# SSD scan: the decay matrix and x as rounded halves, and the state product in the state bank

## The chip, the cores and the metric

The kernel runs on one core of a Trainium2 chip. The metric is the device time of one execution in microseconds (us); lower is better. The chip's engines appear under these names: TensorE (PE; its weight loads are listed apart as PEld), VectorE (DVE), ScalarE (ACT), GpSimd (POOL) and SyncE (SP), whose queue issues most DMAs.

## What is computed

The reference is one inference step of two layers, a Mamba-2 SSD layer and a latent attention (MLA) layer, for a prompt of 1024 tokens and 8 samples of 8 tokens. The change is in the SSD scan of the prompt. For each of 8 groups (4 heads of width 64 and a shared state width of 128) it goes over 8 chunks of 128 tokens. Cut to what matters:

```python
seg = a_cs[..., :, None] - a_cs[..., None, :]
decay = jnp.where(causal, jnp.exp(jnp.where(causal, seg, 0.0)), 0.0)
cb = jnp.einsum('bclgn,bcsgn->bgcls', cc, bc)
y_diag = jnp.einsum('bgrcls,bcsgrp->bclgrp', cb[:, :, None] * decay, xdt)     # inside a chunk
states = jnp.einsum('bcsgn,bcsgrp->bcgrpn', bc, xdt * decay_end[..., None])   # what a chunk adds
# over the chunks:  state -> chunk_decay * state + states[chunk], from prev = the state before it
y_off = jnp.einsum('bclgn,bcgrpn->bclgrp', cc, prev) * decay_in[..., None]    # from earlier chunks
y = y_diag + y_off
```

After it come `y + D * x`, the gate `silu(z)`, a grouped norm and the output projection.

## The kernel before

The SSD layer projects the normalised input to z, x, B, C and dt, convolves x, B and C over time, runs the scan, and multiplies by the output weights. Matrix products that must be as exact as f32 are made of two rounded halves: `split` (L125) copies a tile to fp32r with ScalarE (L127, the high half) and subtracts that from the tile with VectorE or GpSimd (L133, the low half); `mm3` (L83) then adds three matmuls, high by high, high by low and low by high. Some products are left as plain f32 matmuls.

The groups are a pipeline: while the scan of group g runs, the projections and convolution of group g + 1 (`Group.steps`, matmuls `pj` at L86 and `pz` at L98) are issued in between. `layer_ssd` (L926 to L938) asks for the steps in proportion to the scan's progress; `ssd_scan` (L733) mixes chunks and the samples' state updates in the order `SCAN`. In the last group the first half of the output projection (`poa`) takes the place of the next group's projections. In this layer no order is written by hand: the code gives instructions in program order, and a scheduler puts them on the queues of the engines by its own estimate of time. On a queue, an instruction that waits holds up those behind it.

A chunk of `ssd_chunks` (L580) does this:

- transposes x (two blocks) and B into the bank `trp` (L594 to L597); copies x to `xsT` (L599); splits B into `Bh`, `Bl` (L602).
- makes `xdd` = x times decay to the chunk's end on GpSimd (L613) and splits it into `dh`, `dl`; splits C into `Ch`, `Cl` and the state S into `Sh`, `Sl` (L618, L620), with GpSimd for the low halves; makes `xD` = D * x (L622).
- makes the product C·B in the bank `cb` (L624).
- loads the cumulated decay into M by DMA (L626), adds the causal mask on VectorE (L627), takes the exponential for each of 4 heads on ScalarE (L630), and multiplies by C·B on VectorE (L631). M is 128 x 4 x 128.
- multiplies M of each head with 64 columns of x in plain f32 into columns 0 to 255 of the bank `py` (L635).
- adds what the chunk brings to the state in the bank `ps` (L639, columns 0 to 255), and from the second chunk on makes the product of C with the state in columns 256 to 511 of `py` (L644).
- the new state S2 is the decayed S (GpSimd, L645) plus `ps` (VectorE, L647).
- y: the state product times decay (L651), plus the first product (L652), plus `xD` (GpSimd, L653), times z (L656); in the first chunk there is no state product (L655). Then the squares are summed (L657) and y is written out (L658).

The ninth chunk of a group holds the samples (64 tokens, `smp`) and takes its state product from `ssd_states` (L669), which also uses the tags of `M` (tile xr, L685), `fo` (tile xf, L690) and the bank of `ps` (L725). Accumulator banks: `tr` 2, `pj` 2, `cb` 1, `y` 2 (tile py), `st` 1 (tile ps).

Of the kernel before, what the change touches and what calls it, by code (L numbers as in the profile page):

```python
# [8 lines left out]
F32 = mybir.dt.float32  # L9
F32R = mybir.dt.float32r  # L10
AF = mybir.ActivationFunctionType
ALU = mybir.AluOpType
# [70 lines left out]
def mm3(nc, out, pairs):  # L83
    n = len(pairs)
    for i, (a, b) in enumerate(pairs):
        nc.tensor.matmul(out, a, b, start=(i == 0), stop=(i == n - 1))  # L86
# [26 lines left out]
def open_pool(tc, name, bufs=1, space=None, **kw):  # L113
    if space is None:
        return tc.tile_pool(name=name, bufs=bufs, reuse_waits="tile", **kw)
    if space == PS:
        return tc.tile_pool(name=name, bufs=bufs, space=space, reuse_waits="tile", **kw)
    return tc.tile_pool(name=name, bufs=bufs, space=space, **kw)
# [6 lines left out]
def split(k, hi, lo, src, eng=None, parts=0):  # L125
    nc = k.nc
    nc.scalar.copy(hi, src)  # L127
    n = parts and hi.shape[1] // parts
    for a in range(parts):
        s = slice(a * n, a * n + n)  # L130
        (eng or nc.vector).tensor_tensor(lo[:, s], src[:, s], hi[:, s].bitcast(F32), op=ALU.subtract)
    if not parts:
        return (eng or nc.vector).tensor_tensor(lo, src, hi.bitcast(F32), op=ALU.subtract)  # L133
# [446 lines left out]
def ssd_chunks(k, gr, pools):  # L580
    nc, I = k.nc, k.I
    sp, psum = pools
    g = gr.g
    S = None
    hs = slice(4 * g, 4 * g + 4)
    for i in range(9):
        t0, m = TILES[i]
        sl = slice(t0, t0 + m)
        smp = i == 8
        B, C, X0, X1 = (gr.xc[q][1][:, j] if smp else gr.xc[q][0][:, j, sl] for q in range(2) for j in range(2))  # L590
        z = gr.z[i // 5][:m, i % 5]
        tag = f"{g}_{i}"
        p = psum.tile([128, 512], F32, tag="tr", name="trp" + tag, bufs=PB["tr"])
        nc.tensor.transpose(p[:m, 0:128], X0, k.ident)  # L594
        nc.tensor.transpose(p[:m, 128:256], X1, k.ident)
        if not smp:
            nc.tensor.transpose(p[:m, 256:384], B, k.ident)  # L597
        xsT = sp.tile([128, 256], F32, tag="xsT", name="xsT" + tag, bufs=2)
        nc.scalar.copy(xsT[:m], p[:m, 0:256])  # L599
        if not smp:  # L600
            Bh, Bl = (sp.tile([128, 128], F32R, tag="BT" + x, name="BT" + x + tag, bufs=2) for x in "hl")
            split(k, Bh, Bl, p[:, 256:384])  # L602
        tk = k.tok[:m, i]

        def hb(j):
            return tk[:, j, hs].unsqueeze(2).to_broadcast([m, 4, 64])

        def v3(t):
            return t[:m].rearrange("p (h q) -> p h q", q=64)

        if not smp:
            xdd = sp.tile([128, 256], F32, tag="xdd", name="xdd" + tag, bufs=1)
            nc.gpsimd.tensor_tensor(v3(xdd), v3(xsT), hb(2), op=ALU.mult)  # L613
            dh, dl = (sp.tile([128, 256], F32R, tag="xdd" + x, name="xdd" + x + tag, bufs=1) for x in "hl")
            split(k, dh, dl, xdd, nc.gpsimd)
            if S is not None:
                Ch, Cl = (sp.tile([128, 128], F32R, tag="C" + x, name="C" + x + tag, bufs=1) for x in "hl")
                split(k, Ch, Cl, C, nc.gpsimd)  # L618
                Sh, Sl = (sp.tile([128, 256], F32R, tag="S" + x, name="S" + x + tag, bufs=1) for x in "hl")
                split(k, Sh, Sl, S, nc.gpsimd)  # L620
        xD = sp.tile([128, 256], F32, tag="xD", name="xD" + tag, bufs=XDB)
        nc.gpsimd.tensor_tensor(v3(xD), v3(xsT), k.dsk[:m, hs].unsqueeze(2).to_broadcast([m, 4, 64]), op=ALU.mult)  # L622
        pc = psum.tile([128, 512], F32, tag="cb", name="cb" + tag, bufs=PB["cb"])
        nc.tensor.matmul(pc[:m, :m], B, C, start=True, stop=True)  # L624
        M = sp.tile([128, 4, 128], F32, tag="M", name="M" + tag, bufs=2)
        nc.sync.dma_start(M[:m, :, :m], (k.acss_d[hs] if smp else k.acs_d[i, hs]).partition_broadcast(m))  # L626
        nc.vector.tensor_tensor(M[:m, :, :m], M[:m, :, :m],  # L627
                                (k.negs if smp else k.negu)[:m, :m].unsqueeze(1).to_broadcast([m, 4, m]), op=ALU.add)
        for h in range(4):
            nc.scalar.activation(M[:m, h, :m], M[:m, h, :m], AF.Exp, bias=tk[:, 0, 4 * g + h : 4 * g + h + 1])  # L630
        nc.vector.tensor_tensor(M[:m, :, :m], M[:m, :, :m],  # L631
                                pc[:m, :m].unsqueeze(1).to_broadcast([m, 4, m]), op=ALU.mult)
        py = psum.tile([128, 512], F32, tag="y", name="py" + tag, bufs=PB["y"])
        for h in range(4):
            nc.tensor.matmul(py[:m, h * 64 : h * 64 + 64], M[:m, h, :m], xsT[:m, h * 64 : h * 64 + 64],  # L635
                             start=True, stop=True)
        if not smp:
            ps = psum.tile([128, 512], F32, tag="st", name="st" + tag, bufs=PB["st"])
            mm3(nc, ps[:, :256], [(Bh, dh), (Bh, dl), (Bl, dh)])  # L639
            S2 = sp.tile([128, 256], F32, tag="S", name=f"S{g}_{i + 1}", bufs=2)  # L640
            if S is None:
                nc.vector.tensor_copy(S2, ps[:, :256])
            else:
                mm3(nc, py[:m, 256:], [(Ch, Sh), (Ch, Sl), (Cl, Sh)])  # L644
                nc.gpsimd.tensor_tensor(S2.rearrange("p (h q) -> p h q", q=64), S.rearrange("p (h q) -> p h q", q=64),  # L645
                                        k.decp[:, hs, i : i + 1].to_broadcast([128, 4, 64]), op=ALU.mult)
                nc.vector.tensor_tensor(S2, S2, ps[:, :256], op=ALU.add)  # L647
            S = S2
        y = sp.tile([128, 256], F32, tag="y", name="y" + tag, bufs=YB)
        if i:  # L650
            nc.vector.tensor_tensor(v3(y), v3(gr.yo if smp else py[:, 256:]), hb(3), op=ALU.mult)  # L651
            nc.vector.tensor_tensor(y[:m], y[:m], py[:m, :256], op=ALU.add)  # L652
            nc.gpsimd.tensor_tensor(y[:m], y[:m], xD[:m], op=ALU.add)  # L653
        else:
            nc.vector.tensor_tensor(y, py[:, :256], xD, op=ALU.add)  # L655
        nc.vector.tensor_tensor(y[:m], y[:m], z, op=ALU.mult)  # L656
        nc.scalar.activation(xD[:m], y[:m], AF.Square, accum_out=k.yssq[:m, i, g : g + 1])  # L657
        nc.sync.dma_start(k.y_d[sl, 256 * g : 256 * g + 256], y[:m])  # L658
        if i == 7:
            pf = psum.tile([128, 512], F32, tag="tr", name="pf" + tag, bufs=PB["tr"])  # L660
            for pr in range(2):
                nc.tensor.transpose(pf[:, pr * 128 : pr * 128 + 128], S[:, pr * 128 : pr * 128 + 128], k.ident)
            fo = sp.tile([128, 256], F32, tag="fo", name="fo" + tag, bufs=1).rearrange("p (a n) -> p a n", a=2)
            nc.scalar.copy(fo, pf[:, :256].rearrange("p (a n) -> p a n", a=2))
            nc.sync.dma_start(k.O["p_ssm"][0, 0, 4 * g : 4 * g + 4].rearrange("(a h) p n -> (h p) a n", h=2), fo)
        yield
# [66 lines left out]
def ssd_scan(k, gr, pools):  # L733
    chunks, states = ssd_chunks(k, gr, pools), ssd_states(k, gr, pools)
    for c in SCAN:
        next(chunks if c == "c" else states)
        yield 21 / len(SCAN)
    drain(chunks)
    drain(states)
# [125 lines left out]
def layer_ssd(k):  # L865
    tc, nc = k.tc, k.nc
# [7 lines left out]
    with ExitStack() as st:  # L874
# [39 lines left out]
                pass  # L914
            ssd_dt(k, p0, psum)
        sp = right.enter_context(open_pool(tc, name="sp", bufs=2, side="right"))
        k.cblk = [sp.tile([128, 4, 64], F32R, name=f"cblk{q}") for q in range(2)]
        for t in k.cblk:
            nc.gpsimd.memset(t.bitcast(F32), 0.0)
        gr = g0  # L920
# [5 lines left out]
        for g in range(G - 1):  # L926
# [11 lines left out]
            gr = nx  # L938
# [1091 lines left out]
def hybrid_kernel(tc, ins, outs):  # L2030
    k = Ctx()
    k.tc, k.nc, k.I, k.O, k.ng = tc, tc.nc, ins, outs, G
    with ExitStack() as st:
        setup(k, st)
        layer_ssd(k)
        layer_mla(k)
# [19 lines left out]
```

## Time and profile before

| | before |
|---|---|
| median of 3 runs | 1953.28 us (1952.03 to 1955.74) |
| the profiled execution | 1949.75 us |
| span of its instructions | 1948.0 us |
| busy TensorE / VectorE / ScalarE / GpSimd | 97% / 61% / 57% / 43% of the span |
| matmul instructions | 12023 |
| bytes moved by DMA | 202.01 MB, 104 GB/s on average |

The profile is of one execution: its span is the time from the first instruction to the last, and the execution's own time lies 1.75 us above it. Times of rows are microseconds from the span's start, and durations of one instruction stand in ns where they are means of a group. A matmul's recorded duration holds its passage through the array, which overlaps with the next matmul's; what a matmul costs in a row of them is the distance from its start to the next one's. A plain f32 matmul stands as two rows. In a row of grouped instructions, the part behind the bar has the busy time, the mean duration, and the time for which the engine sat idle before them, with what ended it.

### The profile page before, as it was taken

The page shows a single profiled execution, that of the slowest core. Times are in us where ns is not written, and L with a number is a line of the kernel's source. Part 1 is how long each engine was busy: PE and PEld are TensorE (multiplying, and loading weights), DVE is VectorE, ACT ScalarE, POOL GpSimd, SP SyncE. Part 2 cuts the span into 40 slices and gives each one's busy share as a digit, 9 for nine tenths or more (in the row PEclk, how much of TensorE's full clock was granted, in tenths as well). Part 3 has the DMA queues.
Part 4 walks back from the last instruction along what each step waited for, and adds up shares of the span by engine and source line. Part 5 has one row for each costly group of instructions (what it writes and reads, how often), then busy time and mean ns, then how long its engine had stood idle before and what let it go on. Part 6 is the DMA issues. An engine that isn't in the chain of part 4 may idle for free.

```text
span 1948.0 us, 33561 instructions
## 1 busy us (share of the span) xinstructions
PE 1898.6 (97%) x12023; PEld 1732.3 (89%) x12023; DVE 1189.8 (61%) x2423; ACT 1108.4 (57%) x2535; POOL 841.3 (43%) x1122
## 2 busy tenths in 40 slices
PE   9999999999999999899999999999999999899998
PEld 7999999999999999788788998898888888778887
DVE  5566565657666656755533104476787778666564
ACT  6466666667666666732214314336777777855552
POOL 2447455555655555443003212104443434865551
PEclk9999999999999999999999999999999999999999
DMA  5123223332323332544533333133111112654431
GB/s 167 48 72 93 86 85 97 84 108 84 96 81 96 86 95 82 190 161 156 181 114 117 123 150 94 56 109 94 48 49 41 51 40 59 215 181 149 144 128 38
DMA packets 181086, 202.01 MB, mean 104 GB/s; under 512 B 18828, under 2 KB 147608, under 8 KB 180536
## 3 DMA queue, kind: packets, MB, share of 16 engines
q1 hardware_dynamic: 175864, 180.08, 30.1%
q0 software_dynamic: 4976, 19.66, 2.9%
q8 instruction: 95, 1.56, 0.3%
q14 instruction: 71, 0.58, 0.1%
q10 hardware_dynamic: 80, 0.13, 0.0%
HBM read 146.52 MB, written 53.28 MB: 103 GB/s over the span
## 4 chain that ended last, share of the span: by engine, by line
PE 82%; ACT 5%; DMA 4%; DVE 4%; POOL 3%; issue 2%; SPq 0%; POOLq 0%; DVEq 0%; ACTq 0%
PE pj L86 19%; PE pz L98 8%; PE pq L98 6%; PE pob L98 5%; PE p L98 5%; PE poa L98 5%; PE sc L86 2%; PE py L635 2%; PE o L86 2%; DMA M<-acs_d 2%; PE o L1426 2%; PE sc L1363 2%; PE o L1428 2%; PE st L1395 2%; PE st L1397 2%
## 5 line engine op out<-in xcount | busy, mean ns | idle before, releaser
L86 PE MATMUL pj<-xh,wih 128*128 128x384 f32 (+1 forms) x768 | 254.2, 335 | 0.5 <-ACT raw L512 0.3
L86 PE MATMUL pj<-xl,wih 128*128 128x384 f32 (+1 forms) x768 | 253.7, 330 | 0.0
L86 PE MATMUL pj<-xh,wil 128*128 128x384 f32 (+1 forms) x768 | 253.2, 330 | 0.0
L1409 POOL TENSOR_TENSOR tl<-P,th 128x384 fp32r<-128x384 f32 (+1 forms) x96 | 91.3, 951 | 235.1 <-ACT P L1407 188.9
L526 DVE SCALAR_TENSOR_TENSOR acc<-raw,vec,acc 128x1112 f32<-128x1112 f32 x96 | 142.2, 1482 | 26.4 <-ACT acc L522 25.4
L86 PEld LDWEIGHTS pj<-xh,wih 128*128 128x128 f32 x768 | 143.9, 188 | 2.3 <-ACT xh L273 0.8
L86 PEld LDWEIGHTS pj<-xl,wih 128*128 128x128 f32 x768 | 144.5, 188 | 1.0
L86 PEld LDWEIGHTS pj<-xh,wil 128*128 128x128 f32 x768 | 144.4, 188 | 0.4
L98 PE MATMUL pz<-wih,xh 128*128 128x256 f32 x504 | 142.8, 287 | 0.6 <-ACT z L567 0.6
L98 PE MATMUL pz<-wil,xh 128*128 128x256 f32 (+1 forms) x504 | 140.2, 284 | 0.0
L1406 ACT ACTIVATE th<-st 128x512 fp32r<-128x512 f32 x192 | 94.5, 492 | 65.5 <-PE st L1402 50.5
L630 ACT ACTIVATE M<-M,tok 128x128 f32<-128x128 f32 (+1 forms) x288 | 90.9, 386 | 66.7 <-DVE M L627 66.3
L98 PE MATMUL pz<-wih,xl 128*128 128x256 f32 x448 | 128.3, 286 | 0.0
L1699 POOL TENSOR_TENSOR kvl<-pgr,kvh 128x256 fp32r<-128x256 f32 x128 | 96.3, 779 | 66.3 <-ACT kvh L1697 65.6
L98 PEld LDWEIGHTS pz<-wih,xh 128*128 128x128 f32 x504 | 95.9, 190 | 1.3 <-ACT z L567 1.0
L627 DVE TENSOR_TENSOR M<-M,negu 128x512 f32<-128x512 f32 x64 | 52.6, 822 | 68.3 <-DMA M<-acs_d 67.9
L1407 ACT ACTIVATE P<-st 128x512 f32<-128x512 f32 x192 | 93.7, 488 | 0.0
L98 PEld LDWEIGHTS pz<-wil,xh 128*128 128x128 f32 (+1 forms) x504 | 92.7, 184 | 0.7
L133 DVE TENSOR_TENSOR wil<-wraw,wih 128x512 fp32r<-128x512 f32 x88 | 71.3, 817 | 27.6 <-ACT wih L127 24.4
L613 POOL TENSOR_TENSOR xdd<-xsT,tok 128x256 f32<-128x256 f32 x64 | 50.8, 794 | 80.5 <-ACT xsT L599 80.1
L98 PEld LDWEIGHTS pz<-wih,xl 128*128 128x128 f32 x448 | 85.2, 190 | 0.1
L1409 DVE TENSOR_TENSOR tl<-P,th 128x512 fp32r<-128x512 f32 x96 | 70.9, 739 | 18.5 <-ACT P L1407 17.6
(832 smaller groups left out, 6302.7 us busy)
## 6 DMA issues: line engine op xcount, KB each, us to landing
wraw<-in_ssd_w_in SPq DMA_DIRECT2D x92, 256.0 KB
M<-acs_d SPq DMA_DIRECT2D x64, 256.0 KB
s<-in_state_ssm SPq DMA_DIRECT2D x32, 256.0 KB
y_d<-y SPq DMA_DIRECT2D x64, 128.0 KB
out_s_ssm<-s SPq DMA_DIRECT2D x32, 256.0 KB
wraw<-in_ssd_w_out SPq DMA_DIRECT2D x12, 512.0 KB
q_d<-qt SPq DMA_DIRECT2D x32, 192.0 KB
qp<-q_d SPq DMA_DIRECT2D x8, 768.0 KB
```

The costliest lines, as they stand in the source:

```text
L86: nc.tensor.matmul(out, a, b, start=(i == 0), stop=(i == n - 1))
L98: nc.tensor.matmul(o, a, b, start=(j == 0), stop=(j == len(ops) - 1))
L133: return (eng or nc.vector).tensor_tensor(lo, src, hi.bitcast(F32), op=ALU.subtract)
L526: last = nc.vector.scalar_tensor_tensor(acc, raw[:, j : j + n], k.convw[j][:, blk : blk + 1], acc, op0=ALU.mult, op1=ALU.add)
L613: nc.gpsimd.tensor_tensor(v3(xdd), v3(xsT), hb(2), op=ALU.mult)
L627: nc.vector.tensor_tensor(M[:m, :, :m], M[:m, :, :m], (k.negs if smp else k.negu)[:m, :m].unsqueeze(1).to_broadcast([m, 4, m]), op=ALU.add)
L630: nc.scalar.activation(M[:m, h, :m], M[:m, h, :m], AF.Exp, bias=tk[:, 0, 4 * g + h : 4 * g + h + 1])
L635: nc.tensor.matmul(py[:m, h * 64 : h * 64 + 64], M[:m, h, :m], xsT[:m, h * 64 : h * 64 + 64], start=True, stop=True)
L1406: nc.scalar.activation(th[:, :n], ps[:, :n], AF.Exp, scale=SCALE)
L1407: nc.scalar.activation(P[:, :n], ps[:, :n], AF.Exp, scale=SCALE)
L1409: eng.tensor_tensor(tl[:, :n], P[:, :n], th[:, :n].bitcast(F32), op=ALU.subtract)
L1699: nc.gpsimd.tensor_tensor(rl[:, j], raw[:, j], rh[:, j].bitcast(F32), op=ALU.subtract)
```

## The change

For the 64 prompt chunks, M and x are split into rounded halves. The halves of x lie side by side for each head, so that one matmul with 128 moving columns gives M's half times both halves of x; two such matmuls (Mh, Ml) are added up in 128 columns of `py`, which is filled by the four heads. The two column blocks of each head are added when y is made. The product of C with the state goes to the free columns of `ps`, ahead of the chunk's own contribution. `xdd` shares its buffer with `xf` and `fo`, and the two tiles `cblk` get one buffer each instead of two. The samples' chunk is left as it was.

```diff
+            xhl = sp.tile([128, 4, 2, 64], F32R, tag="xhl", name="xhl" + tag, bufs=1)
+            split(k, xhl[:, :, 0], xhl[:, :, 1], p[:, 0:256].rearrange("p (h q) -> p h q", q=64))
...
-            xdd = sp.tile([128, 256], F32, tag="xdd", name="xdd" + tag, bufs=1)
+            xdd = sp.tile([128, 256], F32, tag="fo", name="xdd" + tag, bufs=1)
...
-        for h in range(4):
-            nc.tensor.matmul(py[:m, h * 64 : h * 64 + 64], M[:m, h, :m], xsT[:m, h * 64 : h * 64 + 64],
-                             start=True, stop=True)
+        pv = py.rearrange("p (h a q) -> p h a q", h=4, a=2)
+        if smp:
+            for h in range(4):
+                nc.tensor.matmul(py[:m, h * 64 : h * 64 + 64], M[:m, h, :m], xsT[:m, h * 64 : h * 64 + 64],
+                                 start=True, stop=True)
+        else:
+            Mh, Ml = (sp.tile([128, 4, 128], F32R, tag="M" + x, name="M" + x + tag, bufs=1) for x in "hl")
+            split(k, Mh, Ml, M)
+            for h in range(4):
+                nc.tensor.matmul(py[:, h * 128 : h * 128 + 128], Mh[:, h], xhl[:, h].rearrange("p a q -> p (a q)"),
+                                 start=True, stop=False)
+                nc.tensor.matmul(py[:, h * 128 : h * 128 + 128], Ml[:, h], xhl[:, h].rearrange("p a q -> p (a q)"),
+                                 start=False, stop=True)
...
             ps = psum.tile([128, 512], F32, tag="st", name="st" + tag, bufs=PB["st"])
+            if S is not None:
+                mm3(nc, ps[:, 256:], [(Ch, Sh), (Ch, Sl), (Cl, Sh)])
             mm3(nc, ps[:, :256], [(Bh, dh), (Bh, dl), (Bl, dh)])
...
-                mm3(nc, py[:m, 256:], [(Ch, Sh), (Ch, Sl), (Cl, Sh)])
...
-            nc.vector.tensor_tensor(v3(y), v3(gr.yo if smp else py[:, 256:]), hb(3), op=ALU.mult)
-            nc.vector.tensor_tensor(y[:m], y[:m], py[:m, :256], op=ALU.add)
+            nc.vector.tensor_tensor(v3(y), v3(gr.yo if smp else ps[:, 256:]), hb(3), op=ALU.mult)
+            if smp:
+                nc.vector.tensor_tensor(y[:m], y[:m], py[:m, :256], op=ALU.add)
+            else:
+                nc.vector.tensor_tensor(v3(y), v3(y), pv[:, :, 0], op=ALU.add)
+                nc.vector.tensor_tensor(v3(y), v3(y), pv[:, :, 1], op=ALU.add)
...
-            nc.vector.tensor_tensor(y, py[:, :256], xD, op=ALU.add)
+            nc.vector.tensor_tensor(v3(y), pv[:, :, 0], v3(xD), op=ALU.add)
+            nc.vector.tensor_tensor(v3(y), v3(y), pv[:, :, 1], op=ALU.add)
...
-        k.cblk = [sp.tile([128, 4, 64], F32R, name=f"cblk{q}") for q in range(2)]
+        k.cblk = [sp.tile([128, 4, 64], F32R, name=f"cblk{q}", bufs=1) for q in range(2)]
```

More of the change, by code (lines that the diff above doesn't have):

```diff
@@ L600, in ssd_chunks @@
         if not smp:
+            xhl = sp.tile([128, 4, 2, 64], F32R, tag="xhl", name="xhl" + tag, bufs=1)
+            split(k, xhl[:, :, 0], xhl[:, :, 1], p[:, 0:256].rearrange("p (h q) -> p h q", q=64))
+        if not smp:
             Bh, Bl = (sp.tile([128, 128], F32R, tag="BT" + x, name="BT" + x + tag, bufs=2) for x in "hl")
```

## The prediction

> **What bounds the kernel now.** I read the page first, then busy time by stage, then what TensorE waited for, then its instructions one by one.
>
> ```profile
> PE 1898.6 (97%) x12023; PEld 1732.3 (89%) x12023; DVE 1189.8 (61%) x2423; ACT 1108.4 (57%) x2535; POOL 841.3 (43%) x1122
> ...
> PE 82%; ACT 5%; DMA 4%; DVE 4%; POOL 3%; issue 2%; SPq 0%; POOLq 0%; DVEq 0%; ACTq 0%
> ```
>
> TensorE is busy for 97% of the span and carries 82% of the chain that ended last. A busy TensorE need not be at its peak, so the stage has to be looked at. The changed lines run in the scan, from 117 to 916 us, in three stretches:
>
> ```profile
> core 0 of [0], span 1948.0 us
> core 0: us, PE busy (x) PEld busy (x) DVE busy (x) ACT busy (x) POOL busy (x), PEclk, DMA share, GB/s
> 117.00:220.00 103.00, 97.07 (x723) 94.44 (x721) 70.77 (x118) 69.27 (x175) 66.72 (x93) 1.00 0.35 100
> 220.00:800.00 580.00, 574.49 (x4223) 562.14 (x4221) 374.75 (x621) 391.79 (x959) 324.58 (x478) 1.00 0.31 91
> 800.00:916.00 116.00, 109.99 (x625) 92.38 (x624) 72.13 (x124) 48.59 (x132) 49.00 (x69) 0.99 0.50 171
> ```
>
> TensorE idles 5.9 + 5.5 + 6.0 = 17.4 us in these 799 us; in the middle stretch it is 99% busy, at the full granted clock. VectorE has 65% there, ScalarE 68%, GpSimd 56%. What TensorE waits for between 117 and 916 us, the largest first:
>
> ```profile
> PE st L86 <- POOL xddl L133: 3.6, 2, 2.5
> PE cb L624 <- DVE yo L722: 2.0, 2, 1.0
> PE pv L719 <- DVE sl L133: 2.0, 1, 2.0
> PE sn L726 <- POOL bb L701: 1.9, 5, 0.4
> PE st L86 <- ACT xddh L127: 1.7, 2, 1.4
> ```
>
> No engine holds it back regularly. So a microsecond saved on TensorE in the scan is a microsecond of the whole, one saved elsewhere is nothing, and one added elsewhere is free as long as TensorE has other matmuls in front.
>
> **The change part by part.** First the product with the decay matrix (L635), in 64 full chunks (the 8 sample chunks keep their code). One chunk of before:
>
> ```profile
> 327.98 0.34 PE L86 MATMUL pj<-xh,wil 128*128 128x384 f32 x1
> 328.16 1.00 PE L635 MATMUL py<-xsT,M 128*128 128x64 f32 x8
> 328.96 0.36 PE L86 MATMUL st<-xddh,BTh 128*128 128x256 f32 x1
> 329.17 0.28 PE L86 MATMUL st<-xddl,BTh 128*128 128x256 f32 x1
> 329.28 0.28 PE L86 MATMUL st<-xddh,BTl 128*128 128x256 f32 x1
> ```
>
> Four f32 matmuls stand as 8 passes, each with a weight load of 128 columns. They take 0.80 us from start to start, and the matmul behind them takes 0.21 us where the next one takes 0.11, so 0.10 us more belongs to them: 0.90 us a chunk, 0.11 us a pass. The new code has eight rounded (fp32r) matmuls, Mh and Ml for four heads, also with 128 weight columns each, and 128 moving columns. The trace has such matmuls in the attention:
>
> ```profile
> 1335.72 0.27 PE L1396 MATMUL st<-qTl,kTh 98*128 98x128 f32 x1
> 1335.83 0.27 PE L1397 MATMUL st<-qTh,kTl 98*128 98x128 f32 x1
> 1335.94 0.28 PE L1402 MATMUL st<-mr 128*128 128x128 f32 x1
> 1336.06 0.44 PE L86 MATMUL kp<-kvh,w 128*128 128x512 f32 x1
> ```
>
> They start 0.11, 0.11 and 0.12 us apart, 0.113 on average, no less than the 256 columns wide ones above. Streaming doesn't explain that; the weight load does, because the same width behind narrower weights (32 and 64 columns) goes twice as fast:
>
> ```profile
> 345.87 0.22 PE L719 MATMUL pv<-sl,cblk 128*32 128x128 f32 x1
> 345.93 0.22 PE L719 MATMUL pv<-sh,cblk 128*64 128x128 f32 x1
> ```
>
> Both forms are thus bound by loads, and both have eight: 8 x 0.113 = 0.91 us after, 0.90 before. **This term is 0**; the last digits make it at most 0.02 us a chunk either way, 1.3 us in all. The matmuls of the state products keep number and shape; where they write (state bank, not y bank) costs TensorE nothing.
>
> The Trainium skill's "TensorE: Matmul & The Clock Gate", section Back-to-back issue gap, gives about 81 ns for a sustained pair of a weight load and a 128-column matmul. By it the eight would take 0.65 us, and the sum would be 64 x 0.25 = 16 us lower (estimate). The rows above, at 110 ns, disagree with it for this data type, and I go by them.
>
> Next, what the other engines get, per full chunk. The nearest rows, between 117 and 916 us:
>
> ```profile
> L599 ACT COPY xsT<-trp 128x256 f32<-128x256 f32 x64 | 24.0, 375 | 12.1 <-PE trp L597 11.7
> ...
> L652 DVE TENSOR_TENSOR y<-y,py 128x256 f32<-128x256 f32 x56 | 23.1, 413 | 0.7
> ...
> L133 DVE TENSOR_TENSOR sl<-s0p,sh 128x512 fp32r<-128x512 f32 x32 | 21.9, 685 | 7.0 <-ACT sh L127 6.9
> ...
> L127 ACT CAST sh<-s0p 128x512 fp32r<-128x512 f32 x32 | 18.5, 578 | 0.8 <-PE s0p L710 0.8
> ```
>
> ScalarE: Mh (128x512) 0.58, the high half of x (128x256) 0.38, together 0.96 us. VectorE: Ml 0.68, the low half of x 0.41, one more addition to y 0.41, together 1.50 us. Over 64 chunks: 61 us of ScalarE and 96 us of VectorE. Spread over 799 us, ScalarE goes from 510 to 571 us (71%) and VectorE from 518 to 614 us (77%). Neither becomes the bound on average; the cover is the projection matmuls of the next group, which TensorE runs meanwhile. If that cover were gone, the price would be the latency, below.
>
> The chain to the product grows: L631 (the multiplication with C·B), then Mh, then Ml, then the matmuls, two hops of 0.58 + 0.68 = 1.26 us. How early is M ready now? VectorE's rows, then TensorE's, for a common chunk and for the one with the shortest lead:
>
> ```profile
> 331.44 0.67 DVE L631 TENSOR_TENSOR M<-M,cb 128x512 f32<-128x512 f32 x1
> ...
> 549.56 0.68 DVE L631 TENSOR_TENSOR M<-M,cb 128x512 f32<-128x512 f32 x1
> ```
>
> ```profile
> 334.60 1.00 PE L635 MATMUL py<-xsT,M 128*128 128x64 f32 x8
> ...
> 551.15 1.00 PE L635 MATMUL py<-xsT,M 128*128 128x64 f32 x8
> ```
>
> The leads are 334.60 - 332.11 = 2.49 us and 551.15 - 550.24 = 0.91 us. Of the 64 leads, 7 are under 1.3 us (1.9 us short in all) and 16 under 2.0 us (9.6 us short in all, if 0.7 us of queueing is added to the two hops). The code lets the order of each engine be written anew by the scheduler, and one that knows the longer chain puts the product later, at no cost. So this term lies between 0 and 9.6 us, and I take **5 us**, the middle: rows on both sides are equally near.
>
> The state. Now ps is held through both products and the reading of both halves, in the only buffer of its tag, and B's product stands behind C's, so S_(i+1) waits for Sh and Sl of S_i, which it didn't:
>
> ```profile
> L133 POOL TENSOR_TENSOR Sl<-S,Sh 128x256 fp32r<-128x256 f32 x56 | 51.6, 922 | 4.0 <-ACT Sh L127 4.0
> ...
> L127 ACT CAST Sh<-S 128x256 fp32r<-128x256 f32 x56 | 22.4, 401 | 9.5 <-DVE S L647 9.4
> ```
>
> The loop is 0.40 + 0.92 + two products of 0.33 (three steps of 0.11) + 0.41 for the addition: 2.4 us, against 799 / 64 = 12.5 us a chunk on average and 6 to 7 us where two follow each other (328.16 and 334.60). Hidden; so is the next user of that buffer, L726's matmul, by the projections. In return the first y product no longer stands behind M's matmuls, which helps VectorE, not TensorE. The x halves (one buffer) wait for the previous product and keep the transposes' bank that much longer; ScalarE, where those copies queue, also empties the projections' banks behind them. That, and GpSimd slowed by 64 more two-operand subtractions on VectorE, no row prices; between 0 and the 5.5 us that the middle stretch idles now, I take **1 us**, near the lower end, since the middle stretch shows almost no such wait. The shared tag of xdd, the single buffer of cblk: 0. No DMA is added, and the load of the next M waits for Ml instead of the matmuls behind it, so SP's queue is not later.
>
> Sum: 0 + 5 + 1 = 6 us. The profiled execution took 1949.75 us, so 1955.8; the median of the three runs is 1953.28, so **1959 us**, +0.3%. A measurement of this kernel tells 0.2%, 3.9 us, from no change.
>
> **Rivals.**
> *All of it is covered* (same): the order is rewritten and TensorE's queue stays as full as the 99% now. Then 1953, give or take 3.9. For it: equal loads on TensorE, and a typical lead of 2.5 us. Against it: leads near 1 us.
> *The waits go away* (faster): C's product leaves M's shadow, and the waits for xdd and S, up to 3.6 + 1.7 us, vanish in the new order: 1948. The ceiling is the whole idle time of the scan, 17.4 us: 1936. Against it: nothing is taken from GpSimd, which those waits name.
> *Rounded weights load faster* (faster): at the 0.06 us of the last two TensorE rows the eight would take 0.48 us, 64 x 0.42 = 27 us off, 1926. The attention rows speak against it. By the Trainium skill's figure above it would be 1937.
> *In-order queues block* (slower): at 77% and 71% a copy of Mh that waits for VectorE stands in front of ScalarE's emptying of projection banks. It decides once TensorE is held up at every chunk: one Ml (0.68 us) a chunk is 64 x 0.68 = 44 us, 1997; half the chunks, 1975.
> *The change does nothing for TensorE* isn't a rival but the forecast's own basis.
>
> **How the numbers follow.** Forecast (slower by 4 to 12 us) 0.37, queues block 0.14, all covered 0.31, waits go away 0.14, faster loads 0.04. Slower 0.51, same 0.31, faster 0.18. The range from 1947 to 1983 leaves out the faster loads, the upper part of the vanished waits, and the blocked queues above some two thirds of the chunks, about 0.15; the likeliest case alone is 1957 to 1965.
>
> **What would show it.** Right: L635's successors at eight passes 0.11 us apart; TensorE's busy time in the scan within 1 us of before; waits of the y product for Ml (VectorE) as the new name among TensorE's waits, some 5 us; VectorE near 614 us in the scan. Wrong: starts closer than 0.1 us; waits of pj or pz for ScalarE of over 10 us (queues block); a scan shorter than 799 us with no waits for Ml.

## The result and the profile after

| | before | after |
|---|---|---|
| median of 4 runs each, in turn on one chip | 1952.65 us (1951.14 to 1955.74) | 2005.09 us (1997.36 to 2009.82) |
| ratio to before, 95% interval | | 1.0267 [1.0245, 1.029] |
| the profiled execution | 1949.75 us | 2003.53 us |
| mean granted TensorE clock | 0.996 | 0.986 |

The change makes the kernel 52 us slower; the forecast was 1959 and its range ended at 1983. From the page of the kernel after, the busy times and the chain that ended last:

```profile
PE 1921.4 (96%) x12023; PEld 1748.3 (87%) x12023; DVE 1294.3 (65%) x2615; ACT 1164.8 (58%) x2667; POOL 857.8 (43%) x1122
...
PE 65%; DVE 12%; ACT 11%; DMA 7%; issue 4%; POOL 2%; SPq 0%; DVEq 0%; ACTq 0%; POOLq 0%
```

The number of matmuls is the same, and TensorE still looks 96% busy. But its share of the chain falls from 82% to 65%; VectorE, ScalarE and DMA take what it loses. For a third of the time the chain now runs through something other than TensorE's own work.

**Where the time went.** The first matmul of the output projection's second half starts at 942.0 us before and at 992.8 us after, 50.8 us later; what follows takes 1006 and 1009 us. So the loss is in the scan. The windows view of the scan, before and after (117 us to 26 us ahead of that matmul):

```profile
117.00:916.00 799.00, 781.55 (x5565) 748.95 (x5564) 517.65 (x860) 509.65 (x1265) 440.30 (x639) 1.00 0.35 104
```

```profile
117.00:967.00 850.00, 801.27 (x5560) 762.40 (x5559) 622.06 (x1050) 565.24 (x1395) 455.55 (x638) 0.98 0.33 97
```

The columns are window, length, busy time and instructions of TensorE, its weight loads, VectorE, ScalarE and GpSimd, then the granted clock. TensorE's idle time grows from 799 - 781.55 = 17.5 to 850 - 801.27 = 48.7 us, by 31.3 us. Its busy time grows by 19.7 us with as many matmuls; the last column but two explains most of it: the granted clock fell from 1.00 to 0.98, and 2% of 850 is 17 us. The 2 to 3 us left are not traced to a cause. VectorE grew by 104.4 us (96 were predicted) and ScalarE by 55.6 us (61 were predicted). At 73% and 67% of the window neither is near full.

The product itself, from the timeline of TensorE after:

```profile
412.20 0.28 PE L646 MATMUL py<-xhl,Mh 128*128 128x128 f32 x1
412.32 0.27 PE L648 MATMUL py<-xhl,Ml 128*128 128x128 f32 x1
412.43 0.28 PE L646 MATMUL py<-xhl,Mh 128*128 128x128 f32 x1
412.54 0.27 PE L648 MATMUL py<-xhl,Ml 128*128 128x128 f32 x1
```

The starts are 0.11 us apart, as forecast: eight of them cost 0.9 us, like the eight passes before.

What TensorE waited for, 117 to 967 us after, the largest first:

```profile
PE trp L594 <- ACT fo L683: 9.4, 3, 3.8
PE cb L627 <- DVE yo L741: 4.9, 5, 1.6
PE sn L745 <- POOL bb L720: 3.7, 4, 1.2
PE st L86 <- POOL xddl L133: 3.7, 2, 3.3
PE st L86 <- ACT BTh L127: 3.1, 3, 1.8
PE ytpa L839 <- ACT fo L683: 2.9, 1, 2.9
```

The columns are the wait, its total, how often, and the longest. The reader should note what isn't there: the product with M hardly waits. In the groups of instructions by line, the number behind the second bar is the engine's idle time ahead of them:

```profile
L646 PE MATMUL py<-xhl,Mh 128*128 128x128 f32 x256 | 60.3, 266 | 1.8 <-ACT Mh L127 1.1 <-DVE xhl L133 0.8
...
L648 PE MATMUL py<-xhl,Ml 128*128 128x128 f32 x256 | 58.8, 268 | 0.0
...
L133 DVE TENSOR_TENSOR Ml<-M,Mh 128x512 fp32r<-128x512 f32 x64 | 56.3, 879 | 15.0 <-ACT Mh L127 14.4
...
L127 ACT CAST Mh<-M 128x512 fp32r<-128x512 f32 x64 | 39.7, 621 | 21.5 <-DVE M L634 17.2 <-PE py L646 3.4 <-DVE acc L526 0.7
```

The scheduler did put the product late enough. ScalarE stands 21.5 us in front of Mh and VectorE 15.0 us in front of Ml, and whatever is queued behind them on these engines stands too.

One place shows how such a queue reaches TensorE. From the timeline of all engines after, at the end of a group:

```profile
412.41 1.29 SPq L629 DMA_DIRECT2D M<-acs_d  x1
...
416.70 0.69 DVE L630 TENSOR_TENSOR M<-M,negu 128x512 f32<-128x512 f32 x1 [3.57 <-DMA M<-acs_d]
...
417.47 1.28 ACT L633 ACT_TABLE_LOAD   x1 [5.97 <-DVE M L630]
418.76 1.28 ACT L633 ACTIVATE M<-M,tok 128x128 f32<-128x128 f32 x4
419.95 0.35 ACT L683 COPY fo<-pf 128x256 f32<-128x256 f32 x1
...
420.35 0.47 PE L594 MATMUL trp<-ident,acc 128*128 128x128 f32 x1 [3.78 <-ACT fo L683]
...
422.71 0.52 PE L86 MATMUL pj<-xl,wih 128*128 128x384 f32 x1
423.03 0.52 PE L86 MATMUL pj<-xh,wil 128*128 128x384 f32 x1
423.35 0.52 PE L86 MATMUL pj<-xh,wih 128*128 128x384 f32 x1
```

Read it from below. A transpose waits 3.78 us for ScalarE's copy `fo`, which empties its bank. `fo` needs nothing new, but stands in ScalarE's queue behind an exponential and the table load that goes ahead of it (1.28 us). That load waits 5.97 us for VectorE's mask addition, and VectorE in turn for the load of M, issued at 412.41. The pj matmuls behind the transpose depend on none of this, but TensorE's queue is in order too. Then they start 0.32 us apart, where those before the change are 0.18 apart. The windows view of the eight such stretches of the scan gives the clock:

```profile
256.10:259.50 3.40, 3.40 (x14) 3.37 (x13) 2.93 (x5) 3.34 (x7) 1.04 (x2) 0.50 0.52 142
280.00:283.40 3.40, 3.40 (x18) 3.40 (x18) 3.37 (x5) 1.43 (x6) 2.17 (x3) 0.50 0.11 39
419.90:426.80 6.90, 6.45 (x25) 6.00 (x26) 3.90 (x7) 6.82 (x17) 3.17 (x7) 0.51 0.42 114
...
sum 37.50, PE 35.62 PEld 33.20 DVE 25.43 ACT 32.09 POOL 18.26; mean PE 4.45 PEld 4.15 DVE 3.18 ACT 4.01 POOL 2.28
```

37.5 us at half clock lose some 19 us. Before the change there was one such stretch in the scan, of about 3.4 us, which lost 1.7 us:

```profile
805.60:809.10 3.50, 3.42 (x10) 2.74 (x11) 1.76 (x4) 3.47 (x7) 0.26 (x1) 0.51 0.95 330
```

In sum: 31 us more waiting and 20 us more busy time, some 17 of them the half clock, make the 51 us of the scan. The experiments ask which part of the change causes the waits, and by what.

The table loads in the place above might look like a cause of their own. Before, ScalarE idled 0.4 us in all in front of the exponentials' table loads, and in the kernel after 36.3 us. But two of the versions below (e9 and e10) have 0.5 and 1.9 us there and lose nearly as much, so they aren't what makes the loss.

### The profile page after: what moved, and what is told of

Its sections match the earlier page's. It is cut to its first block, busy times and chain, and to the rows that moved or that the text cites. A ratio compares the mean times of both kernels' runs of the same rounds, so it can differ in the third digit from the quotient of the medians.

```text
span 2001.6 us, 33812 instructions
## 1 busy us (share of the span) xinstructions
PE 1921.4 (96%) x12023; PEld 1748.3 (87%) x12023; DVE 1294.3 (65%) x2615; ACT 1164.8 (58%) x2667; POOL 857.8 (43%) x1122
## 4 chain that ended last, share of the span: by engine, by line
PE 65%; DVE 12%; ACT 11%; DMA 7%; issue 4%; POOL 2%; SPq 0%; DVEq 0%; ACTq 0%; POOLq 0%
PE pj L86 13%; PE pq L98 6%; PE p L98 5%; PE pob L98 5%; PE poa L98 3%; PE pz L98 3%; DMA M<-acs_d 3%; DVE acc L526 3%; PE sc L86 2%; PE o L86 2%; ACT M L633 2%; PE o L1445 2%; PE sc L1382 2%; PE o L1447 2%; PE st L1414 2%
## 5 line engine op out<-in xcount | busy, mean ns | idle before, releaser
L526 DVE SCALAR_TENSOR_TENSOR acc<-raw,vec,acc 128x1112 f32<-128x1112 f32 x96 | 145.5, 1516 | 13.7 <-ACT acc L522 13.1
L133 DVE TENSOR_TENSOR wil<-wraw,wih 128x512 fp32r<-128x512 f32 x88 | 76.7, 876 | 26.3 <-ACT wih L127 23.5
L671 POOL TENSOR_TENSOR y<-y,xD 128x256 f32<-128x256 f32 (+1 forms) x64 | 58.1, 908 | 69.8 <-issue 33.0
```

Source lines behind the costliest of these rows:

```text
L526: last = nc.vector.scalar_tensor_tensor(acc, raw[:, j : j + n], k.convw[j][:, blk : blk + 1], acc, op0=ALU.mult, op1=ALU.add)
```

## The experiments

Three theories stood at the start: the shared buffers (xdd with fo, one buffer for cblk) add waits; the work added to VectorE and ScalarE blocks in-order queues; the order that the scheduler writes anew with each edit has bad places. Each kernel was timed in turn with the kernel before on one chip; differences in us are the ratio less 1, times 1952.65. "Rows that differ" compares the order of TensorE's 12023 matmul rows in two traces, by names and shapes: the fewest rows to be taken out or put in to get from one order to the other. Except in e1 and e2, kernels built on before add work whose result nothing uses.

**1. e1_storage**: before, with the shared buffers only.

```diff
-            xdd = sp.tile([128, 256], F32, tag="xdd", name="xdd" + tag, bufs=1)
+            xdd = sp.tile([128, 256], F32, tag="fo", name="xdd" + tag, bufs=1)
...
-        k.cblk = [sp.tile([128, 4, 64], F32R, name=f"cblk{q}") for q in range(2)]
+        k.cblk = [sp.tile([128, 4, 64], F32R, name=f"cblk{q}", bufs=1) for q in range(2)]
```

> The kernel before with only the two storage edits: xdd shares the buffer of xf and fo, and each cblk tile has one buffer instead of two. Theory 'queued work' (the loss comes from the 1.5 us of VectorE and 0.96 us of ScalarE work added per chunk, which in queues kept in order delays what TensorE needs): within 0.3% of before, 1947 to 1959 us. Rival 'shared buffers' (the waits for the copy to fo, 12 to 13 us in the changed kernel's trace, and the half clock behind them come from the shared tag): 1965 to 1980 us, with waits of transposes for that copy.

Measured 1952.12 us, 0.9999 [0.9981, 1.0017]; 0 rows differ. The buffers cost nothing.

**2. e2_bank**: before, with C's product in the state bank, ahead of B's.

```diff
+            if S is not None:
+                mm3(nc, ps[:, 256:], [(Ch, Sh), (Ch, Sl), (Cl, Sh)])
             mm3(nc, ps[:, :256], [(Bh, dh), (Bh, dl), (Bl, dh)])
-                mm3(nc, py[:m, 256:], [(Ch, Sh), (Ch, Sl), (Cl, Sh)])
```

> The kernel before with only the product of C and the state moved into the free half of the state bank, ahead of B's product; the decay product stays plain f32. Queued work: no work is added, 1947 to 1959 us. Rival 'one state bank': the single buffer is held longer and the state's loop goes through both products, so waits of st and sn grow by 10 us and more: 1963 to 1980 us.

Measured 1963.04 us, 1.0046 [1.0026, 1.0067]: +9 us, with no work added and 1758 rows that differ.

**3. e3_split_m**: before, with Mh and Ml made and not used (and cblk with one buffer, as in e1).

```diff
+        if not smp:
+            Mh, Ml = (sp.tile([128, 4, 128], F32R, tag="M" + x, name="M" + x + tag, bufs=1) for x in "hl")
+            split(k, Mh, Ml, M)
```

> The kernel before, which in addition makes the two rounded halves of M in every full chunk and does not use them (cblk with one buffer, to make room). The product stays plain f32. Queued work: 0.58 us on ScalarE and 0.68 us on VectorE a chunk, about half of the added work, so about half of the loss: 1970 to 1985 us. Shared buffers or one state bank: within 0.3% of before.

Measured 1988.37 us, 1.0176 [1.0144, 1.0208]: +34 us, though no instruction of the chunk needs the halves. TensorE's waits in it:

```profile
PE pz L98 <- ACT z L567: 12.7, 4, 4.2
PE cb L624 <- DVE yo L725: 4.8, 3, 2.4
PE st L86 <- POOL xddl L133: 4.7, 7, 1.3
```

ScalarE's, in the same kernel:

```profile
ACT xD L660 <- DVE y L659: 48.0, 31, 4.3
ACT Mh L127 <- DVE M L631: 40.1, 34, 5.5
```

ScalarE stands 40.1 us in front of an Mh that waits for VectorE; behind it stands, among others, the copy z that empties a projection's bank. So it isn't the longer chain to the product that costs.

**4. e4_split_x**: before, with both halves of x made and not used.

```diff
+            xhl = sp.tile([128, 4, 2, 64], F32R, tag="xhl", name="xhl" + tag, bufs=1)
+            split(k, xhl[:, :, 0], xhl[:, :, 1], p[:, 0:256].rearrange("p (h q) -> p h q", q=64))
```

> The kernel before, which in addition makes the two rounded halves of x from the transposes' bank in every full chunk, ahead of B's halves, and does not use them. Queued work: 0.38 us on ScalarE and 0.41 us on VectorE a chunk, a third of the added work, 1963 to 1975 us. Rival 'transposes' bank' (ScalarE's copy of B waits until VectorE has read x from the same bank): more than its share of work, 1975 us and above. Shared buffers or one state bank: within 0.3% of before.

Measured 1966.40 us, 1.0063 [1.0043, 1.0083]: +12 us. Parts 2, 3 and 4 add up to 55 us, against 52 for the whole change, so that the new matmuls and the buffers need no share. That the sum fits so well is partly luck: each of the two small parts is within the scatter shown below.

**5 to 8. Which half of M's split?** Before, with ScalarE's copy of M alone (e3a), a subtraction of M's size on VectorE alone (e3b), both on VectorE (e3c, with e1's buffers for cblk), and a ScalarE copy of the same size that waits for no other engine, since ScalarE made its source itself (e3d):

```diff
+            nc.scalar.copy(Mh, M)                                        # e3a
+            nc.vector.tensor_tensor(Ml, M, M, op=ALU.subtract)           # e3b
+            nc.vector.tensor_copy(Mh, M)                                 # e3c
+            nc.vector.tensor_tensor(Ml, M, Mh.bitcast(F32), op=ALU.subtract)   # e3c
+            nc.scalar.copy(J, xsT.unsqueeze(1).to_broadcast([128, 2, 256]))    # e3d
```

> The kernel before, which in addition copies M to its rounded high half on ScalarE in every full chunk and does not use it; nothing is added on VectorE. Making both halves cost 34 us. Theory 'ScalarE's queue' (the copy waits there for VectorE's product with C.B, and the emptying of projection banks behind it comes late): most of the 34 us, 1975 us and above. Rival 'VectorE's work' (the subtraction on the busier engine is what costs): under 10 us, below 1964. If both engines' halves simply add up by their length: about 16 us, 1970.

> The kernel before, which in addition makes one subtraction of the size of M's low half (M minus M, 128x512, VectorE, not used) right behind the product with C.B; ScalarE gets nothing. ScalarE's queue: under 10 us, below 1964. VectorE's work: most of the 34 us, 1975 us and above. Halves that add up: about 18 us, 1972.

> The kernel before, which in addition makes both halves of M, unused, but on VectorE alone: the copy moves from ScalarE to VectorE. Theory 'hand-overs' (a subtraction on VectorE alone was free, a copy on ScalarE of VectorE's product cost 12 to 14 us, both 34 us: what costs is a value that goes from one engine's queue to another's and back): 1952 to 1962 us, although VectorE gets more work than in the 34 us case. Rival 'amount of work': 1975 us and above.

> The kernel before, which in addition copies xsT twice into a 128x512 rounded tile on ScalarE, right behind ScalarE's own copy that made xsT, and does not use it: as much ScalarE work as the high half of M, but it waits for no other engine. Hand-overs: 1952 to 1958 us. Rival 'ScalarE's load': the 12 to 14 us of the copy of M again, 1962 to 1968.

| | us | ratio | difference | rows that differ |
|---|---|---|---|---|
| e3a, copy on ScalarE | 1964.47 | 1.0075 [1.0044, 1.0107] | +15 | 400 |
| e3b, subtraction on VectorE | 1953.73 | 1.0002 [0.9985, 1.0018] | 0 | 554 |
| e3c, both on VectorE | 1969.19 | 1.0073 [1.0045, 1.01] | +14 | 1044 |
| e3d, copy on ScalarE, no hand-over | 1980.80 | 1.0119 [1.008, 1.0159] | +23 | 984 |

One subtraction on VectorE, 0.8 us a chunk, is free:

```profile
L636 DVE TENSOR_TENSOR Ml<-M 128x512 fp32r<-128x512 f32 x64 | 52.8, 825 | 0.5
```

A copy on ScalarE is not, with a hand-over or without. That would fit ScalarE's queue as the place, but both halves on VectorE cost as much as the copy. Neither the amount of work nor the number of hand-overs puts all four in order.

**9 to 12. Taking parts of the change back.** The kernel after, without a low half of M (e5: the high half stands in its place, so the output is another one), with Ml on GpSimd (e8), with Mh on VectorE (e9), and with Mh and both halves of x on VectorE, behind B's split (e10):

```diff
-            split(k, Mh, Ml, M)
+            nc.scalar.copy(Mh, M)                                        # e5
+            Ml = Mh                                                      # e5
+            split(k, Mh, Ml, M, nc.gpsimd)                               # e8
+            nc.vector.tensor_copy(Mh, M)                                 # e9, e10
+            nc.vector.tensor_tensor(Ml, M, Mh.bitcast(F32), op=ALU.subtract)   # e9, e10
+            nc.vector.tensor_copy(xhl[:, :, 0], pq)                      # e10
+            nc.vector.tensor_tensor(xhl[:, :, 1], pq, xhl[:, :, 0].bitcast(F32), op=ALU.subtract)   # e10
```

> The changed kernel without M's low half: Mh takes its place in the second matmul of each head, so TensorE has the same eight matmuls and VectorE one subtraction less per chunk (the product is that of a doubled high half). ScalarE's queue: the copy of Mh is still there, so 1990 to 2005 us. VectorE's work: 1970 to 1980 us. Eight weight loads set TensorE's time in any case: the matmuls stay 0.11 us apart.

> The changed kernel with M's low half subtracted on GpSimd instead of VectorE (about 1.4 us a chunk there, by twice the 0.74 us of a 128x256 subtraction). VectorE's work: 1975 to 1990 us, since VectorE is relieved and GpSimd is at 43%. ScalarE's queue: no better than 1995 us.

> The changed kernel with Mh copied by VectorE instead of ScalarE; x is split as in the change. Hand-overs: the 34 us of M's split mostly go, 1970 to 1982 us. Amount of work: VectorE has more of it than in the changed kernel, 2000 us and above.

> As the one before, and both halves of x are made by VectorE, behind B's halves. Hand-overs: the 12 us of x's split go too and the state bank's 9 us stay, 1960 to 1972 us, still slower than the kernel before, since TensorE has gained nothing. Amount of work: above 2005 us.

| | us | ratio to before | against the 52 of after |
|---|---|---|---|
| e5, no low half | 1991.21 | 1.0203 [1.0173, 1.0234] | -12 |
| e8, Ml on GpSimd | 2040.56 | 1.0443 [1.0411, 1.0475] | +34 |
| e9, Mh on VectorE | 1999.98 | 1.0239 [1.0206, 1.0271] | -5 |
| e10, all on VectorE | 1995.43 | 1.0226 [1.0192, 1.026] | -8 |

GpSimd, 43% busy, is the worst place of all. And with all of the new work away from ScalarE (its busy time is 1113.2 us in e10, 1108.4 before), 44 us of loss stay. So ScalarE isn't *the* place either: in e10 the waits have moved to VectorE.

```profile
PE pv L741 <- DVE sl L133: 8.8, 11, 1.3
PE cb L629 <- DVE yo L744: 6.7, 5, 1.4
PE sn L748 <- DVE y L677: 5.2, 3, 2.2
```

**13 to 16. The order alone.** Before, with copies of one single column, next to no work: on VectorE (e12), as ScalarE and VectorE hand-overs at both places of the splits (e17), on ScalarE (e11); and the kernel after with one place mended (e13):

```diff
+            nc.vector.tensor_copy(J, M[:, 0, 0:1])                       # e12
+            nc.scalar.copy(J, M[:, 0, 0:1])                              # e11; e17 has it too
+            nc.vector.tensor_copy(J3, J2)                                # e17, from ScalarE's copy
+            nc.vector.tensor_copy(J, xsT[:, 0:1])                        # e17
+        with k.tc.issue_after(k.foi.ins) if i == 0 and g else nullcontext():   # e13, around the exponentials
```

> The kernel before, with one VectorE copy of a single column of M (128x1, 0.1 us or less) per full chunk, behind the multiplication of M with C.B; its result is used by nothing. The work is next to nothing, but the scheduler's order on TensorE's queue becomes another one in many places. Theory 'load' (what counts is how much work the queues of ScalarE and VectorE hold): 0, at most +2 us. Theory 'new order' (each edit that changes the plan puts some instruction behind one that waits, and this repeats in every group): +5 to +25 us, as the copies of 0.4 to 0.6 us did.

> The kernel before, with three copies of a single column per full chunk: VectorE from xsT, then ScalarE from M and VectorE from ScalarE's result (at the places of the two splits, with the same hand-overs from ScalarE to VectorE, but 128x1 each); their results are used by nothing. Load: 0 to +3 us. New order, or hand-overs by themselves: +10 to +35 us, near the +34 us of the real split of M.

> The kernel before, with one ScalarE copy of a single column of M (128x1) per full chunk, unused. TensorE's, VectorE's and GpSimd's orders stay as they were (but for a few neighbours that are exchanged). Load and new order both expect 0 to +3 us here; more than +5 would say that one more wait in ScalarE's queue costs by itself, whatever its length and the order.

> The kernel after, with the exponentials of a group's first chunk put behind the copy fo of the group before (an order on ScalarE, no wait), so that this copy no longer stands behind an exponential that waits for the load of M. If the few blocked places at a group's end, with the half clock that follows them, are a large part of the loss: 12 to 25 us less than the kernel after, about 1980 to 1993, and no wait of trp or ytpa for fo. If the loss is spread over the load of all chunks: within 6 us of the kernel after, 1999 to 2011; the wait for fo is gone, and others are longer.

| | us | ratio to before | difference | rows that differ |
|---|---|---|---|---|
| e12, one column, VectorE | 1947.92 | 0.9968 [0.9949, 0.9988] | -6 | 174 |
| e17, three columns, with hand-overs | 1968.42 | 1.0074 [1.005, 1.0098] | +14 | 468 |
| e11, one column, ScalarE | 1958.45 | 1.0026 [1.001, 1.0041] | +5 | 16 |
| e13, after with fo first | 2003.46 | 1.0254 [1.0229, 1.0279] | +50 | 986 from after |

"New order" expected +5 to +25 of e12 and it came out faster; "load" expected at most +3 of e17 and it lost 14. Neither theory stands alone: at next to no work the kernel moves by -6 to +14 us. What of the 14 is the order and what the waits of the hand-overs can't be told. Nor are the 6 us seen in the scan: in the profiled execution of e12 it takes 798.7 us, against 799.0 before. e11 keeps the order but for 16 rows and shows what one waiting instruction does to ScalarE's queue:

```profile
L636 ACT COPY J<-M 128x1 f32<-128x1 f32 x64 | 12.5, 196 | 35.8 <-DVE M L631 35.7
```

A copy of one column takes 196 ns, but ScalarE stands 35.8 us in front of them, and the kernel is 5 us slower. e13 removed the waits for `fo`, over 12 us and the half clock behind them, and gained nothing that can be told:

```profile
PE py L641 <- ACT xsT L599: 9.9, 5, 3.1
PE sn L746 <- POOL bb L721: 5.3, 6, 1.2
PE st L86 <- ACT BTh L127: 5.2, 2, 3.4
```

Another tile stands on top, with as much. The place shown above is how a loss happens, not why there is one.

**17 and 18. Work at a fixed order, and after in another order.** e12 again with 128 columns in place of one, which keeps every engine's order; and the kernel after with one unused column copied on VectorE:

```diff
+            nc.vector.tensor_copy(J[:, 0], M[:, 0])                      # e18, on before
+            nc.vector.tensor_copy(J, M[:, 0, 0:1])                       # e19, on after, ahead of the split
```

> As e12_tiny_dve, but the unused copy on VectorE has 128 columns of M instead of one, and every engine keeps the order of e12_tiny_dve, so the two differ by work alone (some 0.1 us of VectorE per full chunk, 7 us in all). If work on VectorE counts only where the order is a bad one: 1946 to 1951, as e12_tiny_dve's 1947.9. If work is what costs: 1952 or more.

> The kernel after, with one unused VectorE copy of a single column of M per full chunk, behind the multiplication with C.B: next to no work, and another order on every queue. It shows how far the order alone moves the kernel after. If the 52 us are the load, with the order as a scatter of some 10 us: 1995 to 2015. If they are a few bad placements that another order would not have: below 1985.

e18: 1945.84 us, 0.9956 [0.9937, 0.9974], -9 us; 0 rows differ from e12's. Its copies, by line:

```profile
L636 DVE COPY J<-M 128x128 f32<-128x128 f32 x64 | 22.3, 349 | 0.5
```

VectorE is busy for 1205.9 us against 1189.6 in e12, 16.3 us more, and the time is no longer. In e19, whose order differs from after's by 1618 rows: 2008.98 us, 1.0283 [1.0252, 1.0314], +55 us. With e13 that makes three orders of the same work at +50 to +55 us. The scatter is real, but the loss isn't made of it.

**Whom TensorE waited for.** For one profiled execution of each, the scan from 117 us to 26 us ahead of the first matmul of the output projection's second half, in us: its length and TensorE's idle time (windows view), the waits added up by the engine that ended them (waits view), and the time at half clock:

| | scan | TensorE idle | for ScalarE | for VectorE | for GpSimd | at half clock |
|---|---|---|---|---|---|---|
| before | 799.0 | 17.4 | 4.4 | 6.2 | 6.6 | 3.4 |
| after | 849.8 | 48.7 | 20.2 | 17.8 | 9.1 | 37.5 |
| e10, all on VectorE | 844.2 | 46.9 | 8.7 | 31.5 | 4.6 | 13.7 |
| e17, three columns, hand-overs | 815.1 | 28.3 | 17.8 | 4.1 | 5.9 | 6.8 |
| e3a, copy on ScalarE | 815.4 | 28.8 | 6.3 | 16.2 | 6.2 | 10.2 |
| e3c, both on VectorE | 819.8 | 28.1 | 9.6 | 5.0 | 12.5 | 6.8 |
| e3d, copy on ScalarE, no hand-over | 825.4 | 36.5 | 9.6 | 17.4 | 9.3 | 17.1 |

With the work on both engines TensorE waits longer for both; with all of it on VectorE, the waits for ScalarE fall by more than half, those for VectorE nearly double, and the sum stays. So e10 gains little: the waits change their engine. In e3a, e3c and e3d it is otherwise: most of TensorE's new waits are not for the engine that got the work. A chain through several queues, like the one shown above, would do that, but it was not followed in these three.

**What is shown, and what stays open.** Shown: the loss is TensorE's waiting plus the half clock behind it. M's split alone, with its halves unused, costs 34 us, so most of the loss needs neither the new matmuls nor the longer chain to them. The shared buffers cost nothing. The loss stays in three orders of the same work, and when all of the work moves to VectorE. A subtraction of 0.8 us a chunk on VectorE is free by itself. Argued, from one place in the trace, from e11 and from the table: the waits come about in queues kept in order, where work that needs nothing new stands behind an instruction that waits. Open: what a given piece of work costs. Kernels with next to no work or little work added lie between -9 and +14 us, so the single differences of 9 to 15 us above (e2, e3a, e3c, e4, and e5, e9, e10 against after) can't be told from that scatter. No version made here is faster than before by its design; e12 and e18 are, by 0.3% and 0.4%, through an order that nobody chose.

## Why the prediction was wrong

- **TensorE's own work, 0**: right. The matmuls start 0.11 us apart, and some 17 of the 19.7 us of added busy time are the clock. So the figure of the Trainium skill that the prediction weighed (81 ns a pair) does not hold here, and "rounded weights load faster" fell.
- **ScalarE +61, VectorE +96 us**: right in size (+56, +104). Ml was 879 ns where the row of a like subtraction had 685, longer only where GpSimd ran beside it (last section); Mh 621 against 578.
- **M's longer chain, 5 us**: the step that failed first, by giving M's split no price but the wait of its own product. The wait was looked for at the product, and there it was 1.8 us. As the prediction said, a scheduler that knows the chain puts the product later; "at no cost" is what was wrong. e3_split_m has the split without any use of it and loses 34 us.
- **x's halves, bank, slower GpSimd, 1 us**: the second mis-sized term. x's split measured 12 us and the bank 9, each within the scatter. It was taken "near the lower end, since the middle stretch shows almost no such wait". That a queue has no waits now says nothing of what it does with 10 to 20% more work in it.
- **The sentence behind both**: an addition elsewhere is "free as long as TensorE has other matmuls in front". They are in front only if they stand ahead in TensorE's own queue. In the place shown above the pj matmuls stood behind a transpose, and 3.78 us passed.
- **The rival "In-order queues block"** had the kind of mechanism and 1997 us, at a chance of 0.14; the median came 8 us above even that. That the price was near is luck: it took TensorE to be held up by an Ml at each of the 64 chunks, while the six largest groups of waits above came 18 times in all and name no Ml. Its sign, waits of pj or pz for ScalarE over 10 us, did not show (under 2 us in all); in e3_split_m it did (12.7). It named one victim, while the queue takes whichever stands behind.
- **Not in the prediction at all: the clock.** 31 us of waits brought some 17 us through the half clock on top, so a microsecond of waiting cost over 1.5. That isn't a fixed price: in e10 29.5 us more waiting brought 10.3 us more at half clock, which loses some 5. The Trainium skill's "TensorE: Matmul & The Clock Gate", section What's actually happening, has the clock at half after an idle window of about 3.4 us, and back at full after as long a busy one. The trace agrees with the length (3.4 us, or twice that) and the factor (0.50), but not with the condition: gaps of 1.79 and 2.18 us were enough, in windows that were not idle (last section).

## What to carry to other kernels

On a TensorE that is 99% busy, work added to other engines is free only where it neither delays what stands behind it in its own queue nor gets TensorE to wait in order; idle shares of 30% don't say so, and neither does a lead of 2.5 us. Read from the trace what is queued behind the new instruction, and price one stall per group with the half clock after it. Where a scheduler writes the order, make a control that adds next to no work: here such kernels moved by -9 to +14 us, and a change of less can't be judged from one build. And where a wait leaves TensorE busy for less than about half of a clock step, add the half clock of the next step (the next section).

## What the runs showed of the hardware

- Gaps of TensorE of 1.8 to 3.8 us were followed by 3.4 us of a granted clock of 0.50, or by 6.8 us, but not each was. From the timeline of TensorE after, the first of these gaps is followed by the half clock from 256.1, and the second by none:

```profile
255.66 0.39 PE L86 MATMUL st<-xddh,BTh 128*128 128x256 f32 x1 [1.79 <-ACT BTh L127]
...
649.71 0.47 PE L745 MATMUL sn<-bb,x 96*128 96x512 f32 x1 [2.61 <-DVE S L657]
```

  A gap's length alone doesn't say whether the clock falls; its place does. The clock changed in fixed steps: the eight stretches in the scan of after begin 0, 7, 48, 80, 143, 166, 175 and 182 times 3.413 us behind the first, at 256.1, and are one or two steps long. The windows view of the steps ahead of the first two stretches, and of the two steps that share the gap of 2.61 us:

```profile
252.70:256.10 3.40, 1.61 (x13) 1.41 (x12) 1.15 (x5) 3.34 (x11) 1.22 (x2) 1.00 0.22 77
276.60:280.00 3.40, 1.22 (x11) 1.15 (x11) 3.27 (x7) 2.09 (x7) 1.89 (x2) 1.00 0.29 77
645.20:648.60 3.40, 1.89 (x13) 1.63 (x11) 1.31 (x4) 2.56 (x5) 2.04 (x2) 1.00 0.42 124
648.60:652.00 3.40, 2.29 (x20) 2.23 (x20) 3.16 (x7) 3.19 (x10) 1.36 (x2) 1.00 0.11 39
```

  TensorE was busy for 47% and 36% of the first two and for 56% and 67% of the others. In all 20 traces, between 110 and 1000 us, each of the 50 steps at full clock with under 45% busy was followed by one at 0.50, and none of the 4875 with over 70%; in between it was 30 of 196. The Trainium skill's "TensorE: Matmul & The Clock Gate", section What's actually happening, has its window run freely, so that a gap's place in it would count; the trace agrees.
- The subtraction that made Ml took 685 ns for one row of before, 825 ns in e3b and 879 ns in the kernel after, each 128 x 512. The trace shows where the rest came from: in the kernel after, the 10 of the 64 that ran with no GpSimd instruction beside them took 676 to 693 ns, the other 54 took 669 to 1586 ns, 915 on average; in e3b it was 681 to 695 ns for 14, and 673 to 1486 for 50. A GpSimd instruction alongside doesn't always lengthen it (17 of the 32 of before had one and took 674 to 692), and which ones do was not separated.
- An fp32r matmul of 128 weight columns and 128 moving columns costs 0.11 us in a row of them, the same as a pass of plain f32 with 64 columns.
